# A small early write of zeros into the output, ahead of the first store, in an add-and-normalise kernel

## The chip, the cores and the metric

The kernel runs on one core of a Trainium2 chip. The metric is device time in microseconds (us).

## The reference

16 x 1024 rows of 512 float32 values are added to a residual and normalised row by row:

```python
z = x + residual
mean = np.mean(z, axis=-1, keepdims=True)
var = np.var(z, axis=-1, keepdims=True)
z_norm = (z - mean) / np.sqrt(var + eps)
return (gamma * z_norm + beta).astype(np.float32)
```

Two tensors of 33.55 MB are read and one is written. There is little arithmetic for each byte.

## The kernel before

Each of the 128 partitions handles 128 rows, called rows 0 to 127 below. They are kept in blocks of 16 that are contiguous in HBM for a partition: 32 KB. `zbuf` holds 64 rows of a partition, `rbuf` 32. SyncE issues every large transfer in the order of a plan: `x48+16` loads rows 48 to 63 of x, `r` is the residual, `o` a store.

```python
PLAN = """
x0+8 r0+8 x8+8 r8+8 x16+16 r16+16 x32+16 r32+16
x48+16 r48+16 o0+16 r64+16 x64+16 o16+16 r80+16 x80+16
o32+16 r96+16 x96+8 x104+8 o48+16 r112+16 x112+8 x120+8
o64+16 o80+16 o96+16 o112+12 o124+4
"""
...
    for kind, lo, n in moves:
        if kind == "x":      # the store of what lay in these rows of zbuf must be over
            while gone < len(stores) and stores[gone][0] < lo + n - Z_ROWS:
                nc.sync.wait_ge(so[gone], 16)
                gone += 1
            move(part(zbuf, Z_ROWS, lo, n), dram(xf, lo, n), ...)
        elif kind == "r":    # the adds that read these rows of rbuf must be over
            wait_rows(s_add, "add", lo + n - R_ROWS)
            move(part(rbuf, R_ROWS, lo, n), dram(rf, lo, n), ...)
        else:
            wait_rows(s_out, "out", lo + n)
            move(dram(of, lo, n), part(zbuf, Z_ROWS, lo, n), ...)
```

POOL adds, ACT takes the mean and the sum of squares of each row (two passes) and the root, and VectorE (DVE) applies rstd (one over that root), gamma and beta in place. gamma and beta come over ACT's own queue and are spread to all partitions by PE. Comments and "..." in the code above are ours.

Of the kernel before, what the change touches and what calls it, by code (L numbers as in the profile page):

```python
# [8 lines left out]
FP32 = mybir.dt.float32  # L9
# [23 lines left out]


EARLY = 2


@with_exitstack
def kernel(
# [9 lines left out]
    nc = tc.nc  # L49
    P = nc.NUM_PARTITIONS  # L50
    xf = x.flatten_outer_dims()
    rf = residual.flatten_outer_dims()
    of = out.flatten_outer_dims()
# [19 lines left out]
    def dram(t, lo, n):  # L73

        b0 = lo - lo % BLOCK
        v = t[P * b0 : P * (b0 + BLOCK), :].rearrange("(p j) d -> p j d", p=P)
        return v[:, lo - b0 : lo - b0 + n, :].rearrange("p a b -> p (a b)")
# [2 lines left out]
    rbuf = nc.alloc_sbuf_tensor("rbuf", [P, R_ROWS * D], FP32)  # L80
    gb_row = nc.alloc_sbuf_tensor("gb_row", [1, 2 * D], FP32)
    ones = nc.alloc_sbuf_tensor("ones", [1, P], FP32)
    eps_t = nc.alloc_sbuf_tensor("eps_t", [P, 1], FP32)
    nm, ssq, std, rstd = (
        [nc.alloc_sbuf_tensor(f"{name}{j}", [P, TURN], FP32) for j in range(SETS)]
# [12 lines left out]
    def sem(name):  # L98
        s = nc.alloc_semaphore(name)
        sems.append(s)  # L100
        return s
# [2 lines left out]
    sx = [sem(f"sx{c}") for c in range(len(loads_x))]  # L104
    sr = [sem(f"sr{c}") for c in range(len(loads_r))]
    s_gb = [sem(f"gb{k}") for k in range(2)]
    s_const = sem("const")
    s_pe = sem("pe")
    s_add = sem("add")
# [8 lines left out]
    def part(buf, size, lo, n):  # L118
        assert lo % size + n <= size
        return buf[:, (lo % size) * D : (lo % size + n) * D]  # L120
# [5 lines left out]
        )  # L126
    nc.vector.memset(ones[:, :], 1.0).then_inc(s_const, 1)  # L127
    nc.vector.memset(eps_t[:, :], float(eps)).then_inc(s_const, 1)  # L128
    nc.tensor.wait_ge(s_const, 1)
    for k, dest in enumerate((gamma_p, beta_p)):  # L130
        nc.tensor.wait_ge(s_gb[k], 16)
# [8 lines left out]
    def wait_rows(s, key, rows):  # L140
        if rows > seen[key]:
            nc.sync.wait_ge(s, rows)
            seen[key] = rows

    def move(out, in_, s):
        i = nc.sync.dma_start(out=out, in_=in_).then_inc(s, 16)  # L146
        if len(first) < EARLY:
            first.append(i.ins)

    gone = 0  # L150
    for kind, lo, n in moves:
        if kind == "x":
# [3 lines that stand above are left out]
            move(part(zbuf, Z_ROWS, lo, n), dram(xf, lo, n), sx[loads_x.index((lo, n))])  # L156
        elif kind == "r":
            wait_rows(s_add, "add", lo + n - R_ROWS)
            move(part(rbuf, R_ROWS, lo, n), dram(rf, lo, n), sr[loads_r.index((lo, n))])
        else:  # L160
            wait_rows(s_out, "out", lo + n)
            move(dram(of, lo, n), part(zbuf, Z_ROWS, lo, n), so[stores.index((lo, n))])

# [9 lines left out]
    lo = 0  # L173
    for n in ADDS:
        for key, loads, s in (("x", loads_x, sx), ("r", loads_r, sr)):
# [5 lines left out]
            out=z, in0=z, in1=part(rbuf, R_ROWS, lo, n), op=ALU.add  # L181
# [11 lines left out]
    with act.Fori(0, total // LAP) as lap:  # L193
        z0 = act.snap((lap * (LAP * D)) % (Z_ROWS * D))
        r0 = act.snap(lap * LAP)
        for j in range(SETS):
# [4 lines left out]
            for k in range(TURN):  # L201
                i = act.activation(  # L202
                    out=junk_m[k][:, :],
                    in_=zk[k],
# [6 lines left out]
            for k in range(TURN):  # L211
                i = act.activation(  # L212
                    out=junk_s[k][:, :],
                    in_=zk[k],
# [7 lines left out]
                out=std[j][:, :],  # L222
                in_=ssq[j][:, :],
# [8 lines left out]
    with dve.Fori(0, total // LAP) as lap:  # L232
        z0 = dve.snap((lap * (LAP * D)) % (Z_ROWS * D))
        r0 = dve.snap(lap * LAP)
        for j in range(SETS):
# [3 lines left out]
            for k in range(TURN):  # L239
                dve.scalar_tensor_tensor(  # L240
                    out=zk[k],
# [9 lines left out]
            for k in range(TURN):  # L251
                i = dve.scalar_tensor_tensor(  # L252
                    out=zk[k],
# [53 lines left out]
```

## Time and profile before

| | before |
|---|---|
| time, median of 3 (range) | 238.73 us (238.37 to 238.76) |
| span of the profiled run | 236.9 us |
| busy: ACT, DVE, POOL, PE | 78%, 75%, 60%, 2% |
| SyncE's DMA queue (q1) | 4176 packets, 100.67 MB, 99.2% of 16 engines' time |
| ACT's DMA queue (q10) | 4 packets (gamma, beta and a semaphore write each) |

Read it from the queues: if one queue fills the 16 DMA engines for 99.2% of the span, the busy shares of the compute engines say little, and the question about a change is what it adds to or takes from the packets' time. The lines themselves are shown and read in the prediction.

A word that is used throughout: a *round* is one large packet on each of the 16 DMA engines. A transfer of 16 rows is eight rounds of 32 KB packets, about 1.21 us each; one of 8 rows is eight rounds of 16 KB packets, 0.61 us each.

### The profile page before, as it was taken

The numbers are of one execution on the slowest core, as the hardware profiler recorded it, in microseconds if no ns is written. First come the engines' busy times: TensorE is split into PE (matmuls) and PEld (weight loads), VectorE is DVE, ScalarE is ACT, GpSimd is POOL, SyncE is SP. The second block draws the span as 40 slices with busy tenths as digits, with TensorE's granted clock in tenths as the row PEclk, the third lists the DMA queues.
The fourth block names the chain that finished last, engine by engine and source line by source line (L and its number), as shares of the span: only waits on it lengthen the run. The fifth ranks groups of instructions, "written<-read, shape, count | busy, mean of one in ns | idle before, by whom it ended". The sixth has DMA issues, their size and how long they took to land.

```text
span 236.9 us, 1471 instructions
## 1 busy us (share of the span) xinstructions
PE 3.7 (2%) x4; PEld 1.2 (0%) x4; DVE 177.2 (75%) x290; ACT 185.5 (78%) x545; POOL 143.0 (60%) x29
## 2 busy tenths in 40 slices
PE   0600000000000000000000000000000000000000
PEld 0100000000000000000000000000000000000000
DVE  0001977939699999999898989896989895698920
ACT  2019879497999999999999998979998956999300
POOL 0098920999799699604995059944995049950000
DMA  8999999999999999999999999999999999999996
GB/s 310 443 432 426 426 443 443 443 443 443 426 415 398 443 443 443 426 420 409 431 437 443 443 443 432 420 407 429 443 437 437 409 432 448 437 420 437 426 430 285
DMA packets 4181, 100.68 MB, mean 425 GB/s; under 512 B 466, under 2 KB 466, under 8 KB 468
## 3 DMA queue, kind: packets, MB, share of 16 engines
q1 hardware_dynamic: 4176, 100.67, 99.2%
q14 instruction: 1, 0.01, 0.0%
q10 hardware_dynamic: 4, 0.00, 0.0%
HBM read 67.11 MB, written 33.55 MB: 425 GB/s over the span
## 4 chain that ended last, share of the span: by engine, by line
DMA 71%; POOL 9%; ACT 9%; DVE 2%; issue 2%; SPq 1%; ACTq 0%; DVEq 0%; POOLq 0%
DMA out_dram<-zbuf 49%; DMA rbuf<-in_residual_dram 16%; POOL zbuf L180 9%; DMA zbuf<-in_x_dram 6%; ACT junk_s L212 5%; ACT junk_m L202 4%; SPq L146 1%; DVE zbuf L240 1%; DVE zbuf L252 1%; ACTq L202 0%; DVEq L240 0%; ACT std L221 0%; DVE rstd L249 0%; ACTq L193 0%; POOLq L177 0%
## 5 line engine op out<-in xcount | busy, mean ns | idle before, releaser
L180 POOL TENSOR_TENSOR zbuf<-zbuf,rbuf 128x2048 f32<-128x2048 f32 (+1 forms) x25 | 142.8, 5740 | 67.6 <-DMA zbuf<-in_x_dram 40.8
L240 DVE SCALAR_TENSOR_TENSOR zbuf<-zbuf,nm,gamma_p 128x512 f32 x128 | 87.1, 743 | 46.3 <-ACT junk_s L212 46.3
L202 ACT ACTIVATE junk_m<-zbuf 128x512 f32 x128 | 74.9, 585 | 29.1 <-POOL zbuf L180 27.5
L212 ACT ACTIVATE junk_s<-zbuf,nm 128x512 f32 x128 | 88.8, 694 | 1.0
L252 DVE SCALAR_TENSOR_TENSOR zbuf<-zbuf,rstd,beta_p 128x512 f32 x128 | 87.1, 743 | 1.1
L212 ACT ACTIVATION_READ_ACCUMULATOR junk_s<-zbuf,nm 128x1 f32 x128 | 23.9, 187 | 0.0
L202 ACT ACTIVATION_READ_ACCUMULATOR junk_m<-zbuf 128x1 f32 x128 | 23.9, 187 | 0.0
L221 ACT ACTIVATE std<-ssq,eps_t 128x4 f32<-128x4 f32 x32 | 9.5, 297 | 3.0
L249 DVE RECIPROCAL rstd<-std 128x4 f32<-128x4 f32 x32 | 5.5, 170 | 0.0
L190 ACT ACT_TABLE_LOAD x1 | 1.3, 1283 | 2.7 <-PEq L60 2.7
L132 PE MATMUL gamma_p<-gb_row,ones 1*128 1x512 f32 x2 | 2.0, 1119 | 7.2 <-DMA gb_row<-in_gamma_dram 7.2
L132 PE MATMUL beta_p<-gb_row,ones 1*128 1x512 f32 x2 | 1.9, 1052 | 0.0
L127 DVE MEMSET ones<- 1x128 f32 x1 | 0.2, 165 | 2.0 <-PEq L60 2.0
L132 PEld LDWEIGHTS beta_p<-gb_row,ones 1*128 1x128 f32 x2 | 0.7, 328 | 1.0 <-issue 0.5
L132 PEld LDWEIGHTS gamma_p<-gb_row,ones 1*128 1x128 f32 x2 | 0.5, 308 | 7.1 <-issue 7.1
L288 POOL MEMSET const-float32-0.0<- 128x1 f32 x1 | 0.1, 98 | 0.2 <-issue 0.2
L288 POOL MEMSET const-bfloat16-1.0<- 128x1 bf16 x1 | 0.1, 101 | 0.0
L288 POOL MEMSET const-uint8-127<- 128x1 uint8 x1 | 0.1, 101 | 0.0
L288 POOL MEMSET const-float32-1.0<- 128x1 f32 x1 | 0.1, 98 | 0.0
L128 DVE MEMSET eps_t<- 128x1 f32 x1 | 0.1, 59 | 0.0
## 6 DMA issues: line engine op xcount, KB each, us to landing
rbuf<-in_residual_dram SPq DMA_DIRECT2D x7, 4096.0 KB, 30.5
out_dram<-zbuf SPq DMA_DIRECT2D x7, 4096.0 KB, 28.6
zbuf<-in_x_dram SPq DMA_DIRECT2D x5, 4096.0 KB, 28.9
zbuf<-in_x_dram SPq DMA_DIRECT2D x6, 2048.0 KB, 14.9
rbuf<-in_residual_dram SPq DMA_DIRECT2D x2, 2048.0 KB, 15.7
out_dram<-zbuf SPq DMA_DIRECT2D x1, 3072.0 KB, 13.5
out_dram<-zbuf SPq DMA_DIRECT2D x1, 1024.0 KB, 10.2
gb_row<-in_gamma_dram ACTq DMA_DIRECT2D x1, 2.0 KB
```

Of the source, the lines that this page charges most:

```text
L127: nc.vector.memset(ones[:, :], 1.0).then_inc(s_const, 1)
L132: nc.tensor.matmul(dest[:, :], ones[:, :], gb_row[:, k * D : (k + 1) * D], start=True, stop=True).then_inc(s_pe, 1)
L146: i = nc.sync.dma_start(out=out, in_=in_).then_inc(s, 16)
L180: nc.gpsimd.tensor_tensor(out=z, in0=z, in1=part(rbuf, R_ROWS, lo, n), op=ALU.add).then_inc(s_add, n)
L190: act.preload_act_table_set("sqrt_and_others")
L202: i = act.activation(out=junk_m[k][:, :], in_=zk[k], func=ACT.Identity, scale=-inv_d, accum_out=nm[j][:, k : k + 1],)
L212: i = act.activation(out=junk_s[k][:, :], in_=zk[k], func=ACT.Square, bias=nm[j][:, k : k + 1], accum_out=ssq[j][:, k : k + 1],)
L221: act.activation(out=std[j][:, :], in_=ssq[j][:, :], func=ACT.Sqrt, bias=eps_t[:, 0:1], scale=inv_d,).then_inc(s_std, TURN)
L240: dve.scalar_tensor_tensor(out=zk[k], in0=zk[k], scalar=nm[j][:, k : k + 1], in1=gamma_p[:, :], op0=ALU.add, op1=ALU.mult,)
L249: dve.reciprocal(out=rstd[j][:, :], in_=std[j][:, :]).then_inc(s_dve, TURN)
L252: i = dve.scalar_tensor_tensor(out=zk[k], in0=zk[k], scalar=rstd[j][:, k : k + 1], in1=beta_p[:, :], op0=ALU.mult, op1=ALU.add,)
L288: nc = _bacc.Bacc("TRN2", target_bir_lowering=False, num_devices=1)
```

## The change

A write of zeros, 64 bytes from each partition, into the first block of the output is issued before any load has landed, and the first store (which overwrites them) waits for that. The intent is to let a cheap write meet early whatever a first write into the output meets.

```diff
+TOUCH = 16
...
+    zeros = nc.alloc_sbuf_tensor("zeros", [P, TOUCH], FP32)
+    s_touch = sem("touch")
...
+    nc.vector.memset(zeros[:, :], 0.0).then_inc(s_const, 1)
+    nc.scalar.wait_ge(s_const, 3)
+    nc.scalar.dma_start(
+        out=dram(of, 0, 1)[:, 0:TOUCH], in_=zeros[:, :]
+    ).then_inc(s_touch, 16)
...
         else:
+            if lo == 0:
+                nc.sync.wait_ge(s_touch, 16)
             wait_rows(s_out, "out", lo + n)
```

## The prediction

> **What bounds the kernel now.** I read the page first: the slices and the DMA queues, then the chain of work that ended last.
>
> ```profile
> DMA  8999999999999999999999999999999999999996
> GB/s 310 443 432 426 426 443 443 443 443 443 426 415 398 443 443 443 426 420 409 431 437 443 443 443 432 420 407 429 443 437 437 409 432 448 437 420 437 426 430 285
> ...
> q1 hardware_dynamic: 4176, 100.67, 99.2%
> ...
> q10 hardware_dynamic: 4, 0.00, 0.0%
> HBM read 67.11 MB, written 33.55 MB: 425 GB/s over the span
> ## 4 chain that ended last, share of the span: by engine, by line
> DMA 71%; POOL 9%; ACT 9%; DVE 2%; issue 2%; SPq 1%; ACTq 0%; DVEq 0%; POOLq 0%
> ```
>
> The 16 DMA engines are busy in every slice, and one queue, the SyncE one, fills 99.2% of their time. ACT (78%), DVE (75%) and POOL (60%) all have room. The chain of waits runs through compute for stretches, but its largest part is transfers, and the DMA has no hole anywhere that a quicker compute step could fill. So the end is set by the sum of packet times on each DMA engine: 100.67 MB at the undisturbed rate of 432 GB/s (below) is 233.0 us of the 236.9 us span; the rest is the opening, before the first packets, and the uneven last landing. Consequence for this change: a microsecond of DMA engine time that is added or saved on all 16 engines moves the end by a microsecond, and a wait elsewhere moves it only if it leaves the queue empty.
>
> Next I cut the busy time into stretches that begin and end with whole rounds of packets (a round: one packet on each engine). Columns: stretch, length, busy time of PE, PEld, DVE, ACT, POOL, clock, DMA share, GB/s.
>
> ```profile
> 60.03:69.75 9.72, 0.00 (x0) 0.00 (x0) 7.71 (x14) 9.56 (x30) 8.77 (x2) 1.00 1.00 432
> 69.75:77.03 7.28, 0.00 (x0) 0.00 (x0) 6.67 (x11) 6.96 (x21) 7.28 (x2) 1.00 1.00 432
> 77.03:79.66 2.63, 0.00 (x0) 0.00 (x0) 2.37 (x4) 2.54 (x9) 1.77 (x1) 1.00 1.07 399
> 79.66:89.34 9.68, 0.00 (x0) 0.00 (x0) 8.78 (x16) 9.23 (x28) 8.67 (x2) 1.00 1.00 433
> 89.34:99.02 9.68, 0.00 (x0) 0.00 (x0) 9.38 (x16) 9.32 (x29) 9.18 (x2) 1.00 1.00 433
> ```
>
> There is one slow place, 399 GB/s from 77.03 to 79.66 us. Its position matters. The first store is issued at 59.78 us behind two loads of 4 MB, each 9.7 us, so its data begin at about 79.7 us. The slow place is thus the last two rounds in front of the first write to the output. The stretches after it, with the first and later stores, run at 433. Its size comes from the DMA view of the two rounds in it against the two rounds before, 74.60 to 77.03 us:
>
> ```profile
> q1 hardware_dynamic: 32, 1.05, 106.6%
> ...
> q1 hardware_dynamic: 32, 1.05, 100.1%
> ```
>
> 106.6% of 2.63 us is 2.80 us per engine, 100.1% of 2.43 us is 2.43 us: the same 32 packets cost 0.37 us more per engine. Presumably that is what the change is after: let a small early write meet whatever the first write meets. So the most that it can win is about 0.37 us of 238.73, or 0.16%.
>
> **What the Trainium skill says.** Three places bear on this.
> - "DMA: Bandwidth & Descriptors", section "Queues, rings and completion order": each engine takes turns between the queues it has work for, packet by packet. The trace agrees as far as it goes: the gamma and beta rows of the ACT queue landed while the SyncE queue was full (PE was released at 7.17 us), without waiting for the loads that had been queued before.
> - "DMA: Bandwidth & Descriptors", section "Specifications": 512 B is the least for line rate, below it the engine reads, modifies and writes. A row of 64 B is under it. The trace before has no small write to HBM, so it neither confirms nor refutes a cost.
> - "HBM Reference", section "Specifications": a core that streams alone measures about 425 GB/s, bounded by its DMA engines. The page here has 425 GB/s over the span, so it agrees. I found nothing there about a first write to a tensor being slow.
>
> **The change, part by part.**
>
> 1. *The memset of zeros and the third wait value.* The timeline has DVE's two memsets at 2.00 (0.17 us) and 2.12 (0.06 us). A third one, 128x16, ends by about 2.3 us. DVE's first real work is at 22.77 us. Cost 0.
>
> 2. *ACT's wait and issue.* ACT issues beta from 2.47 to 2.68 us, later than the third memset ends, so its new wait should find the semaphore set. The issue itself takes 0.2 to 0.5 us, as its neighbours do:
>
> ```profile
> 1.92 0.52 ACTq L124 DMA_DIRECT2D gb_row<-in_gamma_dram  x1
> 2.00 0.17 DVE L127 MEMSET ones<- 1x128 f32 x1 [2.00 <-PEq L60]
> 2.12 0.06 DVE L128 MEMSET eps_t<- 128x1 f32 x1
> ...
> 2.47 0.21 ACTq L124 DMA_DIRECT2D gb_row<-in_beta_dram  x1
> 2.71 1.28 ACT L190 ACT_TABLE_LOAD   x1 [2.71 <-PEq L60]
> ...
> 17.06 0.60 ACT L202 ACTIVATE junk_m<-zbuf 128x512 f32 x1 [13.06 <-POOL zbuf L180]
> ```
>
> The table load moves from 2.71 to about 3.2 us and ends near 4.5, with 12.5 us left before the first activation. Cost 0.
>
> 3. *The transfer.* 128 rows of 64 B on 16 engines are 8 packets each, and a semaphore write each. What a small packet takes can be had from the four packets of the ACT queue, two of 2048 B and two semaphore writes of 4 B. Between 6 and 7.45 us they take 0.8% of 16 engines' time, 0.008 x 16 x 1.45 = 0.186 us, so 93 ns for one row with its semaphore. At 432/16 = 27 GB/s 2048 B need 76 ns, which leaves some 17 ns for two packets, 8.5 ns each. A 64 B packet is then, as an estimate, 2.4 + 8.5 = 11 ns; eight and the semaphore write make 0.10 us per engine. If each cost as much as a whole 2 KB row, 93 ns, it would be 0.74 us. Since the engines are never idle, this adds to the end: +0.1 us, at most +0.7 unless small writes are dear (rival D).
>
> 4. *The first store's wait.* From gamma's issue (done at 2.44) to its landing (7.17) are 4.7 us. The touch is issued by 3.2 us; plus 4.7, plus eight turns beside 16-row loads at no more than 1.22 us each, it lands by 18 us, more likely by 13. The wait stands in front of an issue at 59.78 us. It is met more than 40 us early. Cost 0, and no order of transfers changes.
>
> 5. *The slow place at 77 us.* If it belongs to the first write to the output, it disappears there. Whether it is saved or merely met at about 7 us, in front of the small write, the profile can't tell. The engines are as busy at 7 us as at 77, so a stall of the engine costs the same in both places; it is saved only if the small write can wait while the other queue's packets go on. Between 0 and -0.37 us.
>
> Sum: 238.73 + 0.10 + (0 to -0.37) = 238.46 to 238.83; I take the middle, 238.65.
>
> **The rivals.**
> - **A, saved.** The small write meets the cost alone on its queue, the loads pass it, and the first store runs at 433 GB/s. For it: packets of two queues take turns. Against it: at 77 us it was packets of loads that were slow, not the store's own, so whatever holds the first write holds what runs before it. 238.4 us. Chance 35%.
> - **B, moved.** The stall of 0.37 us comes near 7 us and hits two or three rounds of loads there. For it: the argument just given. 238.8 us. 35%.
> - **C, not concerned.** The slow place isn't the first touch of the output's memory but the first change of an engine from loading to bulk storing, or of this particular 32 KB transfer, and stays at 77 us. Against it: the later changes from load to store show nothing. 238.8 us. 25%.
> - **D, small writes are dear.** Each 64 B row is a read and a write of HBM that holds its engine. At 0.2 us each, the average access time in the skill's HBM page ("HBM Reference", section "Latency"), eight make 1.6 us: 240.3. Only at the 2 us which that section gives for high load would it be 16 us and over the 2% mark. Against it: rows of one engine should overlap. 5%, of which the 2% mark takes a fraction.
> - A wait that takes the removed one's place isn't in question: none is removed, and the added one is long met.
>
> **Range and chances.** A to C span 238.4 to 238.85. The three runs before spread over 0.39 us (238.37 to 238.76), and the DMA engines don't finish together, which shifts by some tenths with any change of the opening. With both added, and a little of D on the upper side: 238.0 to 239.3 for 8 in 10. The 2% mark is 4.77 us away; the win is capped at a tenth of it, so faster 0.01; slower only through D or something unseen, 0.02; within 2%, 0.97.
>
> **What would show each step right or wrong.** The ACT queue should have 4 + 128 + 16 = 148 packets with a share near 0.1% or less of the span (step 3: 16 x 0.1 us of 16 x 237 is 0.04%). ACT's first activation should still be near 17.1 us, and the SyncE queue's list of waits should have none on the touch (steps 2 and 4). The two rounds before the first store's data should run at 432 GB/s in A and B, at 399 in C; the stretch from 6 to 13 us should be slow by 0.1 us in A and C and by about 0.5 us in B. The prediction is wrong if the ACT queue's packets take several microseconds (D), if the first store is issued later than 60 us, or if the time drops by more than 0.5 us, which would mean that the first write costs something that the packets' durations don't show.

## The result, and the profile after

| | before | after |
|---|---|---|
| time, median of 6 (range) | 238.64 us (238.37 to 238.76) | 238.59 us (238.30 to 238.69) |
| span of the profiled run | 236.9 us | 237.4 us |
| ACT's DMA queue (q10) | 4 packets | 148 packets |
| slow rounds before the first store, excess per engine | 0.37 us | 0.44 us |

The ratio is 0.9999, with a 95% interval of 0.9986 to 1.0011. Ratios here are the mean time of one kernel's fast runs over that of the other's of the same rounds, so not quite the ratio of the medians in the table.

The page after shows the same bound, and its chain of waits has the same 71% of transfers. Lines of its second and third parts (slices; queues with packets, MB and share of 16 engines' time):

```profile
DMA  8999999999999999999999999999999999999996
GB/s 310 432 434 445 414 442 442 442 442 442 431 420 425 403 442 442 431 431 403 420 442 436 442 442 436 431 389 433 442 436 436 409 428 456 425 431 425 433 438 268
...
q1 hardware_dynamic: 4176, 100.67, 99.1%
q10 hardware_dynamic: 148, 0.01, 0.0%
```

ACT's queue has exactly the 148 packets that were expected, and their time rounds to nothing. What they cost the loads shows in the stretches of the opening. Each stretch below moves 128 packets of 16 KB, from one landing to the next on the first engine. First after, then before (length, busy times, clock, DMA share, GB/s):

```profile
6.57:11.48 4.91, 3.75 (x4) 1.16 (x4) 0.00 (x0) 0.00 (x0) 0.00 (x0) 1.00 1.02 429
11.48:16.35 4.87, 0.00 (x0) 0.00 (x0) 0.00 (x0) 0.00 (x0) 3.85 (x1) 1.00 1.01 431
```

```profile
6.63:11.49 4.86, 3.75 (x4) 1.16 (x4) 0.00 (x0) 0.00 (x0) 0.00 (x0) 1.00 1.01 432
11.49:16.36 4.87, 0.00 (x0) 0.00 (x0) 0.00 (x0) 0.00 (x0) 4.03 (x1) 1.00 1.01 431
```

The load beside which the touch ran took 4.91 us instead of 4.86: the touch cost 0.05 us. The next one took 4.87 in both.

The timeline after shows where the touch and the first store stand (start, duration, queue or engine, line, what):

```profile
2.73 0.40 ACTq L136 DMA_DIRECT2D out_dram<-zeros  x1
...
3.16 1.28 ACT L202 ACT_TABLE_LOAD   x1 [3.16 <-DVE zeros L134]
...
17.23 0.60 ACT L214 ACTIVATE junk_m<-zbuf 128x512 f32 x1 [12.78 <-POOL zbuf L192]
...
59.56 0.33 SPq L156 DMA_DIRECT2D rbuf<-in_residual_dram  x1
60.01 0.36 SPq L156 DMA_DIRECT2D out_dram<-zbuf  x1
```

The table load moved by 0.45 us and is long over when ACT starts at 17.23. The list of DMA issues gives 9.7 us from the touch's issue to its landing, so it was there at 12.4 us. The first store was issued at 60.01 us; SyncE's list of waits after (line, waited for, us in all, times, longest) has seven entries and none for the touch; the three longest:

```profile
SPq L156 <- POOL zbuf L192: 93.9, 6, 27.6
SPq L156 <- DMA out_dram<-zbuf: 74.3, 4, 21.1
SPq L156 <- DVE zbuf L264: 46.0, 3, 21.9
```

That leaves the slow place. The stretches after that answer to the first four of the five of before:

```profile
59.98:69.69 9.71, 0.00 (x0) 0.00 (x0) 7.70 (x15) 9.55 (x30) 8.57 (x2) 1.00 1.00 432
69.69:76.98 7.29, 0.00 (x0) 0.00 (x0) 6.89 (x12) 6.97 (x21) 7.29 (x2) 1.00 1.00 432
76.98:79.77 2.79, 0.00 (x0) 0.00 (x0) 2.33 (x4) 2.70 (x10) 1.97 (x1) 1.00 1.03 376
79.77:89.46 9.69, 0.00 (x0) 0.00 (x0) 8.80 (x16) 9.24 (x28) 8.67 (x2) 1.00 1.00 433
```

It is still there, at the same place, with 376 GB/s in the two rounds before the first store. Its size, by the DMA view of these two rounds and of the two before:

```profile
q1 hardware_dynamic: 32, 1.05, 103.2%
...
q1 hardware_dynamic: 32, 1.05, 100.3%
```

103.2% of 2.79 us is 2.88 us per engine, 100.3% of 2.43 us is 2.44 us. The excess is 0.44 us; before it was 0.37.

So the touch neither saved nor moved what it was aimed at, and cost 0.05 us, an eighth of the distance between the fastest and the slowest of its six runs. What is the slow place, if not the first write to this memory?

### The profile page after: what moved, and what is told of

Same layout as the page of the kernel before. It is cut to its first block, busy times and chain, and to the rows that moved or that the text cites. A ratio compares the mean times of both kernels' runs of the same rounds, so it can differ in the third digit from the quotient of the medians.

```text
span 237.4 us, 1474 instructions
## 1 busy us (share of the span) xinstructions
PE 3.7 (2%) x4; PEld 1.2 (0%) x4; DVE 177.3 (75%) x291; ACT 185.5 (78%) x545; POOL 143.1 (60%) x29
## 3 DMA queue, kind: packets, MB, share of 16 engines
q1 hardware_dynamic: 4176, 100.67, 99.1%
## 4 chain that ended last, share of the span: by engine, by line
DMA 71%; POOL 9%; ACT 9%; DVE 2%; issue 2%; SPq 1%; ACTq 0%; DVEq 0%; POOLq 0%
DMA out_dram<-zbuf 49%; DMA rbuf<-in_residual_dram 16%; POOL zbuf L192 9%; DMA zbuf<-in_x_dram 6%; ACT junk_s L224 5%; ACT junk_m L214 4%; SPq L156 1%; DVE zbuf L252 1%; DVE zbuf L264 1%; ACTq L214 0%; DVEq L252 0%; ACT std L233 0%; DVE rstd L261 0%; ACTq L205 0%; POOLq L189 0%
```

## The experiments

Eleven runs were made (the labels skip e7). Comments in the diffs are ours. Where no rounds of comparison are named, it was one look: a profile, a check of the result and one time. All results were correct. A measure that can be taken in all of them alike: the time that the load in front of the first store takes from the landing of the transfer before it to its own, as the mean of the 16 engines' landings in the packet records. The load x48 of the kernel before takes 9.71 us by it, and r48, in front of the first store, 10.09.

### e1: the touch on SyncE's own queue

Perhaps each queue pays at its own first write, and ACT's touch can't help SyncE's stores.

```diff
-    nc.scalar.wait_ge(s_const, 3)
-    nc.scalar.dma_start(out=dram(of, 0, 1)[:, 0:TOUCH], ...)
...
     for kind, lo, n in moves:
+        if kind == "x" and lo == 16:
+            nc.sync.wait_ge(s_const, 3)
+            nc.sync.dma_start(out=dram(of, 0, 1)[:, 0:TOUCH], ...)
```

> The same touch, issued by SyncE on its own queue between the loads r8 and x16, so that its packets are due at about 21 us. Theory Q (the slow rounds belong to the first write that this queue makes): they move to some 18 to 22 us and the rounds around 78 us run at 432 GB/s. Theory B (they belong to the first bulk store, and 64 B are too little to set them off): two rounds with about 0.4 us of excess per engine stay at 77 to 80 us. Theory T (a place in the run or in the queue's ring, not a store): they stay as well. In all three the time is within 0.5 us of before.

Measured: 238.20 us in one run. The 64 B packets lie at 21.06 to 21.60 us in the packet records, and no large packet is late there. The stretches:

```profile
76.90:79.72 2.82, 0.00 (x0) 0.00 (x0) 2.42 (x4) 2.73 (x10) 1.95 (x1) 1.00 1.00 372
79.72:89.38 9.66, 0.00 (x0) 0.00 (x0) 8.76 (x16) 9.21 (x28) 8.73 (x2) 1.00 1.01 434
```

The first of these lines is the two rounds, the second the first store itself. The load r48 took 10.09 us, as before. Theory Q falls: a 64 B write on the same queue, through the same 16 engines, to the same block changes nothing.

### e2 and e5: the first store earlier, and later

Both without a touch; they ask whether the slow rounds belong to the first store at all, or to a place in time.

```diff
 # e2
-x0+8 r0+8 x8+8 r8+8 x16+16 r16+16 x32+16 r32+16
-x48+16 r48+16 o0+16 r64+16 ...
+x0+8 r0+8 x8+8 r8+8 x16+16 r16+16 o0+8 x32+16 r32+16
+x48+16 r48+16 o8+8 r64+16 ...
```

```diff
 # e5
-x48+16 r48+16 o0+16 r64+16 ...
+x48+16 r48+16 r64+16 o0+16 ...
```

> No touch; the first store is cut in two and its first 8 rows are issued right behind r16, so that their data follow the load that lands at about 40.6 us. Theories Q and B: the slow rounds move with it, to about 38 to 41 us, and the rounds around 78 us run at 432 GB/s. Theory T: they stay at 77 to 80 us. The time is within 1 us of before in all.

> No touch; the first store is issued behind the load r64, so that its data begin one load of 4 MB later, at about 89.5 us. Theories Q and B: the slow rounds are at about 87 to 89.5 us. Theory T: at 77 to 80 us.

Measured in e2 (238.73 us, one run): the stretches before and at the place where the first store's data now begin, and around 78 us.

```profile
30.80:38.04 7.24, 0.00 (x0) 0.00 (x0) 4.43 (x8) 6.61 (x20) 0.29 (x1) 1.00 1.00 430
38.04:41.37 3.33, 0.00 (x0) 0.00 (x0) 3.29 (x7) 3.30 (x11) 0.00 (x0) 1.00 1.00 315
...
75.20:77.63 2.43, 0.00 (x0) 0.00 (x0) 2.41 (x4) 2.43 (x7) 2.43 (x2) 1.00 1.00 432
77.63:80.05 2.42, 0.00 (x0) 0.00 (x0) 1.84 (x3) 2.33 (x8) 2.42 (x1) 1.00 1.00 433
```

Measured in e5 (243.53 us, one run), the last round at full rate and the two rounds before the first store's data:

```profile
86.56:87.77 1.21, 0.00 (x0) 0.00 (x0) 1.21 (x3) 1.21 (x5) 1.21 (x1) 1.00 1.00 433
87.77:91.14 3.37, 0.00 (x0) 0.00 (x0) 2.77 (x5) 3.28 (x10) 3.37 (x2) 1.00 1.01 311
```

In both, the slow rounds moved with the first store: to 38 to 41 us and to 88 to 91 us. Around 78 us e2 runs at 432. Theory T falls by e2; around 80 us e5 is no clean witness, as said below. The size isn't fixed, though: two rounds took 3.33 and 3.37 us instead of 2.43, an excess of 0.9 us, more than twice what it is in the kernels before and after. The second half of the first block in e2 (o8, at 85 us) showed none.

The 5 us that e5 lost in time are another matter. With the store later, x64 waits for it until 101.8 us, and the queue runs dry: x64 takes 13.31 us, with slow rounds of its own. And r64 was issued so late (done at 79.2 us) that its first round began some 0.3 us after r48 had ended and ran 0.8 us over: r64 takes 11.77 us, of which 0.97 are the slow rounds. It is a warning about the plan: the store is early for a reason.

### e3: sixteen times as many small packets

What does a small write cost, and when does the wait begin to bite?

```diff
-        out=dram(of, 0, 1)[:, 0:TOUCH], in_=zeros[:, :]
+        out=dram(of, 0, BLOCK).rearrange("p (a b) -> p a b", a=BLOCK)[:, :, 0:TOUCH],
+        in_=zeros[:, :].rearrange("p (a b) -> p a b", a=BLOCK),
```

> The touch of ACT's queue with 64 B of every row of the first block, 2048 packets in place of 128, so 128 on each engine. If the 11 ns that a packet's record shows is all that it costs, the end moves by 128 x 11 ns = 1.4 us against before (0.6%): about 240.0 us. If a small write costs more than its record shows, a read and a write of HBM say, the end moves by several us. If small packets slip in between others for nothing, the time is that of before. The touch lands at about 90 us if one packet at a time takes turns with packets of 0.6 to 1.2 us, and the first store then waits for it from 60 us on.

Measured, five rounds: 241.82 us against 238.36, ratio 1.0151 (1.0137 to 1.0165). That is 3.5 us, more than the 1.4 us of the packets' records. SyncE's waits, and the stretch in which the first store was issued:

```profile
SPq L157 <- DMA out_dram<-zeros: 21.1, 1, 21.1
```

```profile
80.00:82.00 2.00, 0.00 (x0) 0.00 (x0) 1.97 (x5) 1.97 (x7) 1.22 (x1) 1.00 0.27 25
```

The touch took 78.4 us to land, since an engine takes one 64 B row, then one large packet, in turn: between landings some 144 small packets went with 128 large ones and 16 semaphore writes. The last 670 or so of the 2048 ran alone, from 80.1 to 80.6 us, once the loads had ended; so it landed before the 90 us that were expected. The first store waited 21.1 us for it, was issued at 81.20 us, and by then the queue had run dry: 25 GB/s between 80 and 82 us. When work resumed, late rounds appeared at 90 to 92 us and 110 to 112 us, 0.9 and 0.8 us of excess per engine by the packet records. The second place is in front of a store (o16), as in the other runs. The first isn't: it is the last round of the first store itself, in front of the load r64. That round begins at 90.59 us, and the DMA view from 90.58 to 92.26 us holds it alone:

```profile
q1 hardware_dynamic: 16, 0.52, 114.3%
```

114.3% of 1.68 us is 1.92 us for a round that takes 1.21 elsewhere; the rest of the 0.9 us is in the round after. The first round of this store, begun at 82.04 us out of the dry queue, was only 0.03 us over. So here they went with a change from store to load, and a bulk write that began with no loads in front didn't bring them at its start (one profile). The dry queue and what followed explain most of the loss, and the small packets little: five loads between 21 and 70 us took 48.72 us instead of 48.52, with nine small packets for each engine in each load. 0.20 us over 45 packets is 4 ns each. In the three loads before, with 16 KB packets, it was 0.18 us over 27, 7 ns each. A record shows 11 ns.

### e6 and e12: the same packets, with the wait moved to the last store

```diff
-        out=dram(of, 0, BLOCK)...
+        out=dram(of, 7 * BLOCK, BLOCK)...
...
-            if lo == 0:
+            if lo == 7 * BLOCK:
                 nc.sync.wait_ge(s_touch, 16)
```

> The 2048 packets of e3_many_small, but into the last block of the output, whose store is the one that waits for them, so that the queue can't run dry at the first store. If the 3.4 us of e3_many_small were the wait and the dry queue, only the packets' own cost stays: 128 per engine at the 3.7 to 7 ns by which loads were spread apart in e3_many_small make 0.5 to 0.9 us, at the 11 ns of their records 1.4 us. So 238.9 to 239.8 us; 241 us or more would mean that the wait wasn't the cause.

Measured, five rounds: 239.34 us against 238.55, ratio 1.0032 (1.0008 to 1.0057). This is 0.8 us for 128 packets and a semaphore write per engine, about 6 ns each, within the range written down for the packets alone. But it is net of the slow rounds, which nearly vanished (below): with their 0.3 us added it would be 1.1 us, 8 to 9 ns each, and the interval of the net alone runs from 0.2 to 1.4 us. The other 2.7 us of e3 are then put down to the wait and its consequences.

The stretches held a surprise. Two earlier rounds, and the two rounds before the first store:

```profile
75.12:77.55 2.43, 0.00 (x0) 0.00 (x0) 1.90 (x3) 2.34 (x9) 2.43 (x1) 1.00 1.01 432
77.55:79.98 2.43, 0.00 (x0) 0.00 (x0) 2.36 (x4) 2.43 (x8) 1.68 (x1) 1.00 1.02 432
```

The slow rounds are nearly gone: the load r48 took 9.78 us. The same kernel again, as e12:

> e6_small_unwaited once more. Theory W: excess under 0.1 us at 76 to 82 us again. Theory R: 0.3 to 0.5 us. In both, the loads up to 70 us take 3 to 8 ns more for each small packet that takes its turn between them, as in e3_many_small.

Measured: 239.01 us in one run, 9.85 us for r48. So it was hardly chance that they were small here, though not zero: of these times 9.745 us is what a load takes beside small packets (x48 in both), which leaves 0.03 us of excess per engine in e6 and 0.11 in e12, as in the packet records.

### e4: a touch of 2 KB from each partition

```diff
-TOUCH = 16
+TOUCH = 512
```

> The touch of ACT's queue with a whole row of 2 KB from each partition instead of 64 B (128 packets, 0.26 MB). By their record of 84 ns the eight packets of an engine cost 0.67 us. Theory L (64 B are too little, 512 B and more count as a write): the slow rounds leave 77 to 80 us and show up at 7 to 12 us or not at all. Theory B (only full-size packets of a store count): some 0.3 to 0.5 us of excess per engine stay at 77 to 80 us, and the time is about 0.5 us over before.

Measured: 238.92 us in one run, against 238.55. r48 took 10.07 us, as before. Rows over 512 B make no difference to the slow rounds, so theory L falls for sizes up to 2 KB. Whether it is the size of a packet or the amount of data that makes a write count is not separated: e8 below has packets of 16 KB, and eight times the data. The load beside this touch took 5.46 us instead of 4.87: 0.6 us for eight packets of 2 KB, 74 ns each, near the 84 ns of their record. Here a record is close to the cost; for 64 B it is about double.

### e8: a bulk write on ACT's queue

```diff
-    nc.scalar.wait_ge(s_const, 3)
+    nc.scalar.wait_ge(sr[0], 16)
     nc.scalar.dma_start(
-        out=dram(of, 0, 1)[:, 0:TOUCH], in_=zeros[:, :]
+        out=dram(of, 0, 8), in_=part(rbuf, R_ROWS, 0, 8)
     ).then_inc(s_touch, 16)
...
+            if lo == R_ROWS:   # r32 overwrites rbuf: it waits for this write
+                nc.sync.wait_ge(s_touch, 16)
```

> A bulk early write on ACT's queue: once r0 has landed (11.5 us), 8 rows of it, 16 KB from each partition and 2.1 MB in all, go into the first block of the output as they are (overwritten later by the first store, so the result stays right). It costs 2.1 MB at 432 GB/s, 4.9 us, which is meant. Theory B: the excess comes at about 12 to 20 us, where this write begins, and the rounds before the first store run at 432 GB/s. Theory S (only a change of the SyncE queue from loads to stores counts, whatever other queues have written): the excess stays in the two rounds before the first store, now at about 82 to 85 us.

Measured: 244.03 us in one run, of which 4.9 us were meant. The bulk write's packets begin at 16.89 us. The stretches: four rounds before it, the rounds next to it, and the two rounds before the first store (whose data begin at 85.2).

```profile
11.87:14.31 2.44, 0.00 (x0) 0.00 (x0) 0.00 (x0) 1.28 (x1) 1.75 (x1) 1.00 1.01 430
14.31:16.94 2.63, 0.00 (x0) 0.00 (x0) 0.00 (x0) 0.00 (x0) 2.63 (x1) 1.00 1.07 299
...
82.79:85.22 2.43, 0.00 (x0) 0.00 (x0) 1.96 (x3) 2.34 (x9) 2.04 (x1) 1.00 1.00 432
```

The slow rounds came to the bulk write at 14 to 17 us, with 1.0 us of excess per engine by the packet records, and the first store found none: r48 took 9.71 us. So theory S falls and theory B stands. In all runs but e3, e6 and e12 the slow rounds stand in front of the first bulk write, whether SyncE's or ACT's queue issues it; in after, e1 and e4 the first write to the memory came long before them. (e3 has them also in front of a load, as told above.) The cost can be moved, but was at least as large in the three runs that moved it: here 4.9 us of writing, plus 1.0, less the 0.4 saved later, make the 5.5 us by which this one run was longer.

### e9: the kernel before again

> The kernel before once more, for a second look at the slow rounds: excess of 0.3 to 0.5 us per engine at 77 to 80 us, as seen so far (0.36 before, 0.44 after, 0.34 with the touch on SyncE's queue), no matter whether the touch is there. If it varies by more than 0.2 us from run to run, the difference of 0.08 us between before and after says nothing.

Measured: 238.35 us; r48 took 10.10 us (10.09 in the first profile). The excess is steady enough: 0.38 and 0.39 us in the two runs of before and 0.44 after by this measure, and the 0.06 between them is not worth a reading.

### e10 and e11: small packets at the change, and before it

e6 suggested a kernel that might beat both: a few small packets under way just when the first store begins. ACT's loop is split, and after three laps (e10) or one (e11) it issues 384 packets of 64 B into the last block, which is stored at the end and waits for them.

```diff
+ROWS = 3
+AFTER = 3        # 1 in e11
...
-    with act.Fori(0, total // LAP) as lap: ...
+    act_laps(0, AFTER)
+    act.wait_ge(s_const, 3)
+    act.dma_start(out=dram(of, 7 * BLOCK, ROWS)...[:, :, 0:TOUCH], ...)
+    act_laps(AFTER, total // LAP)
```

> In e6_small_unwaited, where 64 B writes were still under way while the queue changed from loads to the first store, the slow rounds were missing (0.03 us of excess). Here ACT issues 384 such packets (24 for each engine, 3 rows of the last block) after its third lap, at about 58 us, so that they are under way from some 62 to 91 us. Theory W (small writes of another queue that are under way at the change prevent the slow rounds): no excess anywhere between 70 and 90 us, and the time is 0.36 us less for that and 0.1 to 0.2 us more for the packets, so 0.1 to 0.3 us below before (within what five rounds can just see). Theory R (their absence in e6_small_unwaited was chance): 0.3 to 0.5 us of excess at 77 to 80 us.

> The control for e10_small_at_store: the same 384 packets, issued after ACT's first lap at about 29 us and so over by about 63 us, before the change. Both theories: 0.3 to 0.5 us of excess at 77 to 80 us; theory W has this run 0.3 to 0.4 us slower than e10_small_at_store, theory R as fast.

Measured, five rounds each, beside before at 238.43: e10 238.60 us, ratio 1.0016 (1.0001 to 1.0031); e11 239.20 us, ratio 1.0039 (1.0026 to 1.0052). In e10 the small packets ran from 61.4 to 89.1 us, across the change, and r48 still took 10.20 us; in e11 they were over by 59.6 us, and it took 10.06. Theory W falls. No version came out of this that beats either kernel. Why the slow rounds nearly vanish in e6 and e12, where small packets had run beside the loads from the start, stays open.

e11 was slower than e10 by 0.6 us by their medians, though the two intervals overlap. Theory W had 0.3 to 0.4 us, but by slow rounds that e10 was to lack and didn't, so they don't explain it. e11's packet records show what was late in its profiled run. In its last transfer 15 engines landed by 236.3 us and one at 237.4; this one fell back by 0.6 us at 137.9, by 0.8 us at 167.0 and by less elsewhere, each time in a packet next to a change between loads and stores. The other profiles have the same in smaller doses. After 82 us, packets that are over 60 ns late number 5 in the first profile of before, 16 in the second and 25 in the profile of after, mostly one or a few engines of the 16 at a time, and nearly all within two rounds of such a change (about 108, 118, 137, 147, 167, 176 and 196 us). The kernel ends with its slowest engine: its last landing was 0.8 us behind the next engine's in the first profile of before, 0.5 in the second, 0.8 after and 1.1 in e11.

### All together

| run | early write | r48, or the load in front of the first bulk write: excess per engine |
|---|---|---|
| before, e9 | none | 0.38, 0.39 us |
| after | 128 x 64 B, ACT's queue | 0.44 us |
| e1 | 128 x 64 B, SyncE's queue | 0.38 us |
| e4 | 128 x 2 KB, ACT's queue | 0.36 us |
| e10, e11 | 384 x 64 B at, and before, the change | 0.49, 0.35 us |
| e6, e12 | 2048 x 64 B from 7 to 132 us | 0.06, 0.14 us |
| e2, e5 | none; first store earlier, later | 0.9, 0.9 us, moved with it |
| e8 | 2.1 MB, ACT's queue | 1.0 us at that write, none at the first store |

For the runs up to e12 the excess is the load's time minus the 9.71 us of x48 in the kernel before, so that of e6, e12 and e10 includes 0.03 us and more for the small packets beside the load; for e2, e5 and e8 it is that of two rounds or of the packet records, as told above. e3 has no such row: its queue was dry in front of the first store.

## Why the prediction was right

The measured 238.59 us is inside the range, and 0.06 us from the number. So close a hit is luck: the forecasts of A, B and C (238.4 to 238.8) all lie inside the range and hardly further apart than the six runs (238.30 to 238.69), so the time can't tell the mechanisms apart, and half of a saving that didn't come was in the number. The profiles and experiments have to. Point by point:

**The bound.** Right. The queue's share stayed at 99.1%. e8 agrees that added engine time moves the end: 5.5 us for 4.9 of writing and 0.6 of slow rounds.

**Step 1, the memset.** Right: 0.07 us at 2.13 us, no effect.

**Step 2, ACT's issue.** Right: 0.40 us, table load over at 4.44 us. ACT's first activation came at 17.23 us instead of 17.06, since the last of the engines landed r0 0.16 us later; this didn't matter.

**Step 3, the transfer.** Right in kind, half in size. The packets' records show just the 11 ns of the estimate, but what they took from the loads was 0.05 us instead of 0.10, and e3 has 4 to 7 ns for each packet, e6 about 6 by its time as it stands. The term that was too large is the record's length taken as cost: a 64 B packet beside a large one on another queue costs about half of its record. Rival D, whose 0.2 us for each small write was an estimate and not a measured cost, is out.

**Step 4, the wait.** Right: landed at 12.4 us, forecast "more likely by 13". One sign named in the prediction was crossed by a hair: the first store was issued at 60.01 us, where "later than 60 us" was to prove it wrong. The load before it was issued 0.15 us later, and the extra wait instruction took some 0.08 us of SyncE's time (0.45 us from issue to issue instead of 0.37). The store's turn on the engines came at about 79.8 us, so it cost nothing. e3 shows what the same wait does when the touch is long: 21.1 us of waiting, a dry queue, and most of 3.5 us.

**Step 5, the slow place.** This is the step that failed, though it is too small for the time to show. It said: "If it belongs to the first write to the output, it disappears there", and gave A and B, which share that premise, 70%. The runs show C, which was given 25%. e1, e4 and after exclude the first touch of this memory, from either queue, by rows of 64 B or 2 KB; e2, e5 and e8 show that it goes with the first bulk write, through either queue. C's own sign, slow rounds that stay in front of the first store, came true (376 GB/s). The argument against C, that "the later changes from load to store show nothing", wasn't in the lines that it was read from: the stretch 79.66 to 89.34 us is the first store and 89.34 to 99.02 us the load r64, while the second store's data begin at 109 us. (So "the first and later stores" is a wrong reading too.) Stretches of 9.7 us also average 16 engines; in the packet records the later changes cost single engines 0.1 to 0.8 us. And a cost that all engines pay only at the first change would show nothing later. Step 5's sum was then 0 instead of a half of 0.37: steps 3 and 5 together give 238.73 + 0.05 = 238.78. A median of 238.59 doesn't contradict that, given that six runs spread over 0.4 us.

**The size that was claimed as the most to win.** Right as a bound: no touch could have won more than 0.37 us, 0.16%. e8 shows that even a write that does meet the cost early pays 1.0 us for it there. That this is about the same for any early bulk write is not shown; e2's 0.9 us agrees.

**What stays open.** Why all 16 engines lose time at the first change, and later only some do. Engines in step isn't the answer by itself: in e11 the engines' packets before the change were spread over 0.78 us of a 1.21 us round, and 15 of the 16 lost over 60 ns. In e5 the queue ran dry later on, and the first change after that cost the engines again (two rounds from 110.5 to 114.2 us, about 1 us by the packet records). That might suggest that it comes once after each idle spell, but e3 paid twice after one dry stretch, first at a change from store to load and then at one from load to store. No run was made for this alone. And e6's near absence of it has no explanation.

## What to carry to other kernels

When one queue keeps the DMA engines busy, weigh an idea first by the slow place that it is aimed at: here 0.37 us of 238.6 could be had at most, less than the scatter of the end, which one late engine of sixteen sets. A first-time cost that shows in front of the first store need not be a first touch of memory; move the store, and write a little elsewhere, before you build a remedy for one cause. And a wait on a small transfer is free only while that transfer is short: rows of one queue go out one for each large packet of the other, so that their number more than their bytes decides when they land: eight rows for each engine took 9.7 us from issue to landing at 64 B (after) and 10.5 us at 2 KB (e4), 128 rows of 64 B took 78.4 us (e3).

## What the Trainium skill lacked or had wrong

- "DMA: Bandwidth & Descriptors", section "Queues, rings and completion order", has engines change queue after a packet of typically 9 to 17 descriptors. For this touch the turn was one 64 B row: 144 small packets beside 128 large ones and 16 semaphore writes for each load, and 78.4 us until 128 rows per engine had landed (e3).
- The same page, section "Specifications", has writes under 512 B read, modified and written. No run here shows such a cost as added time: a 64 B row to HBM has a record of 11 ns and took 4 to 7 ns from the loads beside it (after, e3), while a 2 KB row took 74 ns (e4). That such a row is far from line rate does show: 64 B in 7 ns are 9 GB/s, against 27 for an engine's large packets (432/16).
- No page tells of the cost of the first change from loads to bulk stores: 0.35 to 1.0 us per engine, on 15 or all of the 16, in the rounds just before the first write's data, whether SyncE's or ACT's queue issues it (in e6 and e12 only 0.03 and 0.11 us, which stays unexplained; in e3 also 0.9 us at a change from store to load); nor that later changes cost single engines up to 0.8 us (e11). The last of 16 engines ended 0.5 to 1.1 us behind the next (before, e9, after, e11).
